# First transfer in two steps, last row but one halved, last row as 512, 256, 256, one semaphore for two sums

## The chip, the cores and the metric

One core of one Trainium2 chip. The time is the device time of one execution in microseconds (us), a median over executions. The profile covers a *span*: from the start of the first recorded instruction of the program to the end of its last. The device time is longer than the span (by 1.35 us in the kernel before); the traces below show semaphore updates that run on after the kernel's last instruction (to 1.46 us after it). The difference between the two is called "the rest" below. A *semaphore* is a counter by which engines and transfers wait for one another, and a transfer has *landed* when its data are in the core's memory (read here from the first instruction on it). Results list spans to 0.1 us, so a single value of the rest is good to about 0.05 us.

## The reference

```
x: (32, 512, 1024) float32
out[b, s] = sum over d of max(x[b, s, d], 0)        # (32, 512) float32
```

67.1 MB are read and 0.07 MB are written, with one comparison and one addition per element.

## The kernel before

The input is seen as 128 partitions by 128 rows of 1024 elements. Seven transfers of 16 rows (8 MiB) come through three buffers. Then 8, 4, 2 and 1 rows come, and at the end the last row in three pieces. For transfers 0 to 5 ScalarE applies relu in place to a step of several rows, and VectorE sums the step with one reduction. For transfer 6 and the tail the two engines take whole rows alternately; each computes relu and sum in one instruction with an accumulator.

```python
STEPS = [4, 5, 7]            # rows of a step, transfers 0 to 4
MIXED = [3, 4, 5]            # transfer 5; its other 4 rows are done whole
TAIL = [8, 4, 2, 1]
LAST = [576, 256, 192]       # pieces of the last row
...
    for c in range(NBIG + 1):
        if c >= NB:                                   # buffer free again?
            sp.wait_ge(s_dve, 3 * (c - NB + 1))
        ...                                           # sp.dma_start(transfer c)
...
    for c in range(NTWO):                             # relu on ScalarE, sum on VectorE
        b, steps = c % NB, STEPS if c < NTWO - 1 else MIXED
        act.wait_ge(s_in[c], 16)
        ...
        for i, n in enumerate(steps):
            t = buf[:, b, r : r + n, :]
            act.activation(t, t, AF.Relu).then_inc(s_act, 1)
            dve.wait_ge(s_act, 3 * c + i + 1)
            dve.tensor_reduce(out=res[...], in_=t, axis=X, op=ALU.add).then_inc(s_dve, 1)
...
    for r, n, s in tail:                              # whole rows, alternately
        if n > 1:
            act.wait_ge(s, 16)
        dve.wait_ge(s, 16)
        for i in range(r, r + n):
            f = on_act if (i - r) % 2 else on_dve
            f(buf[:, tb, i, :], res[:, j0 + i : j0 + i + 1])

    n = LAST[2]
    act.wait_ge(s_in[-3], 16)
    on_act(parts[0], last[:, n : n + 1]).then_inc(s_tact, 1)
    dve.wait_ge(s_in[-2], 16)
    on_dve(parts[1], last[:, n + 1 : n + 2]).then_inc(s_tpart, 1)
    dve.wait_ge(s_tpart, 1)
    dve.wait_ge(s_in[-1], 16)
    dve.wait_ge(s_tact, 1)
    on_dve(last[:, :], res[:, J - 1 : J]).then_inc(s_tdve, 1)   # third piece + both sums
```

Of the kernel before, what the change touches and what calls it, by code (L numbers as in the profile page):

```python
# [2 lines left out]

P = 128
D = 1024
BIG = 16
NTWO = 6
NB = 3
REGIONS = [112, 16]
CHUNKS = [(0, 0), (0, 16), (0, 32), (0, 48), (0, 64), (0, 80), (0, 96)]  # L10
STEPS = [4, 5, 7]
MIXED = [3, 4, 5]
TAIL = [8, 4, 2, 1]
LAST = [576, 256, 192]


def bass_relu_sum_kernel(
    nc: bass.Bass,
    x: bass.AP,
    out: bass.AP,  # L20
):







    fp32 = mybir.dt.float32
    ALU = mybir.AluOpType  # L30
    AF = mybir.ActivationFunctionType
    X = mybir.AxisListType.X

    B, S, _ = x.shape
    J = B * S // P
    NBIG = len(CHUNKS)
    assert BIG * NBIG + sum(TAIL) + 1 == J == sum(REGIONS) and sum(LAST) == D

    xr = x.rearrange("b s d -> (b s) d")
    of = out.rearrange("b s -> (b s)")  # L40
    start = [sum(REGIONS[:i]) for i in range(len(REGIONS))]
    xv = [
        xr[P * s : P * (s + n), :].rearrange("(p j) d -> p j d", p=P)
        for s, n in zip(start, REGIONS)
    ]
    ov = [of[P * s : P * (s + n)].rearrange("(p j) -> p j", p=P) for s, n in zip(start, REGIONS)]

    buf = nc.alloc_sbuf_tensor("buf", [P, NB, BIG, D], fp32)
    last = nc.alloc_sbuf_tensor("last", [P, LAST[2] + 2], fp32)
    res = nc.alloc_sbuf_tensor("res", [P, J], fp32)  # L50

    n_in = NBIG + len(TAIL) + len(LAST)
    s_in = [nc.alloc_semaphore(f"s_in{i}") for i in range(n_in)]
    s_act = nc.alloc_semaphore("s_act")
    s_dve = nc.alloc_semaphore("s_dve")
    s_fact = nc.alloc_semaphore("s_fact")
    s_fdve = nc.alloc_semaphore("s_fdve")
    s_tact = nc.alloc_semaphore("s_tact")
    s_tpart = nc.alloc_semaphore("s_tpart")
    s_tdve = nc.alloc_semaphore("s_tdve")  # L60
    s_store = nc.alloc_semaphore("s_store")
    s_out = nc.alloc_semaphore("s_out")

    sp, act, dve = nc.sync, nc.scalar, nc.vector


    tb = NBIG % NB


    code = nc.main_func.blocks[0].instructions  # L70
    arrival = next(
        i
        for i, ins in enumerate(code)
        if ins.engine == mybir.EngineType.SP and type(ins).__name__ == "InstDrain"
    )
    for c in range(NBIG + 1):
        if c >= NB:
            sp.wait_ge(s_dve, 3 * (c - NB + 1))
        if c < NBIG:
            g, j = CHUNKS[c]  # L80
            sp.dma_start(out=buf[:, c % NB, :, :], in_=xv[g][:, j : j + BIG, :]).then_inc(
                s_in[c], 16
            )
        if c == 0:
            code.insert(arrival, code.pop())
    r = 0
    tail = []
    for i, n in enumerate(TAIL):
        sp.dma_start(out=buf[:, tb, r : r + n, :], in_=xv[-1][:, r : r + n, :]).then_inc(  # L89
            s_in[NBIG + i], 16  # L90
        )
        tail.append((r, n, s_in[NBIG + i]))
        r += n
    n0, n1 = LAST[0], LAST[0] + LAST[1]
    parts = [buf[:, tb, r, 0:n0], buf[:, tb, r, n0:n1], last[:, 0 : LAST[2]]]
    for k, (lo, hi) in enumerate([(0, n0), (n0, n1), (n1, D)]):
        sp.dma_start(out=parts[k], in_=xv[-1][:, BIG - 1, lo:hi]).then_inc(
            s_in[NBIG + len(TAIL) + k], 16
        )
    sp.wait_ge(s_fact, 1)  # L100
    sp.wait_ge(s_fdve, 1)
    for g in range(len(REGIONS) - 1):
        sp.dma_start(
            out=ov[g][:, :], in_=res[:, start[g] : start[g] + REGIONS[g]]
        ).then_inc(s_store, 16)


    def on_act(t, acc):
        return act.activation(t, t, AF.Relu, accum_out=acc)  # L109

    def on_dve(t, acc):
        return dve.tensor_scalar(  # L112
            out=t, in0=t, scalar1=0.0, scalar2=None, op0=ALU.max, op1=ALU.add, accum_out=acc
        )

    def row(c, i):
        return buf[:, c % NB, i, :], res[:, c * BIG + i : c * BIG + i + 1]

    for c in range(NTWO):
        b, steps = c % NB, STEPS if c < NTWO - 1 else MIXED  # L120
        act.wait_ge(s_in[c], 16)
        if steps is MIXED:
            dve.wait_ge(s_in[c], 16)
            for i in (BIG - 4, BIG - 3):
                on_dve(*row(c, i))
        r = 0
        for i, n in enumerate(steps):
            t = buf[:, b, r : r + n, :]
            act.activation(t, t, AF.Relu).then_inc(s_act, 1)  # L129
            dve.wait_ge(s_act, 3 * c + i + 1)  # L130
            dve.tensor_reduce(  # L131
                out=res[:, c * BIG + r : c * BIG + r + n], in_=t, axis=X, op=ALU.add
            ).then_inc(s_dve, 1)
            r += n
        if steps is MIXED:
            for i in (BIG - 2, BIG - 1):
                on_act(*row(c, i))


    j0 = NBIG * BIG  # L140
    for c in range(NTWO, NBIG):
        act.wait_ge(s_in[c], 16)
        dve.wait_ge(s_in[c], 16)
        for i in range(BIG):
            ins = (on_act if i % 2 else on_dve)(*row(c, i))
            if i >= BIG - 2:
                ins.then_inc(s_fact if i % 2 else s_fdve, 1)
    for r, n, s in tail:
        if n > 1:
            act.wait_ge(s, 16)  # L150
        dve.wait_ge(s, 16)
        for i in range(r, r + n):
            f = on_act if (i - r) % 2 else on_dve
            f(buf[:, tb, i, :], res[:, j0 + i : j0 + i + 1])

    n = LAST[2]
    act.wait_ge(s_in[-3], 16)
    on_act(parts[0], last[:, n : n + 1]).then_inc(s_tact, 1)
    dve.wait_ge(s_in[-2], 16)
    on_dve(parts[1], last[:, n + 1 : n + 2]).then_inc(s_tpart, 1)  # L160
    dve.wait_ge(s_tpart, 1)
    dve.wait_ge(s_in[-1], 16)
    dve.wait_ge(s_tact, 1)  # L163
    on_dve(last[:, :], res[:, J - 1 : J]).then_inc(s_tdve, 1)


    sp.wait_ge(s_tdve, 1)
    sp.dma_start(out=ov[-1][:, :], in_=res[:, start[-1] : J]).then_inc(s_out, 16)
    sp.wait_ge(s_store, 16 * (len(REGIONS) - 1))
    sp.wait_ge(s_out, 16)  # L170


# [1 line left out]
_INS = ['x']  # L174
_OUTS = [((32, 512), 'float32')]


# [21 lines left out]
```

## Time and profile before

| what | value | where it is read |
|---|---|---|
| device time | 161.24 us (161.21 to 161.25, 3 executions) | results |
| span | 159.88 us | trace |
| the rest, time less span, same execution | 161.23 - 159.88 = 1.35 us | worked out |
| share of the input queue | 97.9% of 16 DMA engines' span | page, DMA queues |
| landing of the seventh transfer | 137.94 us | timeline, first instruction on it |
| last store issued | 158.41 us | timeline |

The stream of input fills the DMA engines (97.9% of their span).

The timeline of the kernel before from 156.3 us (start, duration, engine, line, operation, output and input, in square brackets the idle time before it and what ended it):

```profile
156.32 1.22 DVE L112 TENSOR_SCALAR_CACHE_REDUCE buf<-buf 128x1024 f32<-128x1024 f32 x1
157.08 0.68 ACT L109 ACTIVATE buf<-buf 128x576 f32<-128x576 f32 x1 [0.90 <-DMA buf<-in_x_dram]
157.47 0.08 DVE L112 DVE_READ_ACCUMULATOR buf<-buf 128x1 f32 x1
157.47 0.41 DVE L112 TENSOR_SCALAR_CACHE_REDUCE buf<-buf 128x256 f32<-128x256 f32 x1
157.67 0.19 ACT L109 ACTIVATION_READ_ACCUMULATOR buf<-buf 128x1 f32 x1
157.81 0.08 DVE L112 DVE_READ_ACCUMULATOR buf<-buf 128x1 f32 x1
158.02 0.36 DVE L112 TENSOR_SCALAR_CACHE_REDUCE last<-last 128x194 f32<-128x194 f32 x1
158.30 0.08 DVE L112 DVE_READ_ACCUMULATOR last<-last 128x1 f32 x1
158.41 0.34 SPq L168 DMA_DIRECT2D out_dram<-res  x1
```

And the last pieces of the chain of waits (start, duration, what):

```profile
122.28 34.02 DMA buf<-in_x_dram
156.30 0.02 issue
156.32 1.57 DVE buf L112 x4
157.89 0.01 issue
157.90 0.05 DVEq L163
157.95 0.07 issue
158.02 0.36 DVE last L112 x2
```

What to see: the last row but one is worked on by VectorE alone for 1.15 us while ScalarE is idle for 0.90; then the sums of the first two pieces end at 157.86 (ScalarE) and 157.89 (VectorE), a separate wait instruction follows at 157.90, and the last addition starts at 158.02.

### The profile page before, as it was taken

The numbers are of one execution on the slowest core, as the hardware profiler recorded it, in microseconds if no ns is written. First come the engines' busy times: TensorE is split into PE (matmuls) and PEld (weight loads), VectorE is DVE, ScalarE is ACT, GpSimd is POOL, SyncE is SP. The second block draws the span as 40 slices with busy tenths as digits, with TensorE's granted clock in tenths as the row PEclk, the third lists the DMA queues.
The fourth block names the chain that finished last, engine by engine and source line by source line (L and its number), as shares of the span: only waits on it lengthen the run. The fifth ranks groups of instructions, "written<-read, shape, count | busy, mean of one in ns | idle before, by whom it ended". The sixth has DMA issues, their size and how long they took to land.

```text
span 159.9 us, 148 instructions
## 1 busy us (share of the span) xinstructions
DVE 122.0 (76%) x58; ACT 101.0 (63%) x55; POOL 0.2 (0%) x4
## 2 busy tenths in 40 slices
DVE  0000006989879897998969989699899999598995
ACT  3000059990699808996099941999339980496972
POOL 0000000000000000000000000000000000000000
DMA  7996996996996997989979969969969969899993
GB/s 262 525 525 262 525 525 262 525 525 262 525 492 295 525 459 328 525 377 410 525 312 476 525 262 525 525 262 525 525 262 525 525 262 525 385 402 394 414 407 116
DMA packets 2305, 67.18 MB, mean 420 GB/s; under 512 B 512, under 2 KB 768, under 8 KB 1024
## 3 DMA queue, kind: packets, MB, share of 16 engines
q1 hardware_dynamic: 2304, 67.18, 97.9%
q14 instruction: 1, 0.01, 0.0%
HBM read 67.11 MB, written 0.07 MB: 420 GB/s over the span
## 4 chain that ended last, share of the span: by engine, by line
DMA 69%; ACT 18%; DVE 11%; SPq 1%; issue 0%; DVEq 0%
DMA buf<-in_x_dram 69%; ACT buf L129 18%; DVE res L131 10%; DVE buf L112 1%; SPq L89 1%; DVE last L112 0%; DVEq L163 0%
## 5 line engine op out<-in xcount | busy, mean ns | idle before, releaser
L131 DVE TENSOR_REDUCE res<-buf 128x4 f32<-128x4096 f32 (+3 forms) x18 | 100.4, 5604 | 33.6 <-ACT buf L129 33.6
L129 ACT ACTIVATE buf<-buf 128x4096 f32<-128x4096 f32 (+3 forms) x18 | 80.8, 4553 | 46.3 <-DMA buf<-in_x_dram 46.3
L109 ACT ACTIVATE buf<-buf 128x1024 f32<-128x1024 f32 (+1 forms) x18 | 18.4, 1024 | 9.8 <-DMA buf<-in_x_dram 9.8
L112 DVE TENSOR_SCALAR_CACHE_REDUCE buf<-buf 128x1024 f32<-128x1024 f32 (+1 forms) x19 | 21.3, 1173 | 2.7 <-DMA buf<-in_x_dram 2.5
L109 ACT ACTIVATION_READ_ACCUMULATOR buf<-buf 128x1 f32 x18 | 3.4, 186 | 0.0
L129 ACT ACT_TABLE_LOAD x1 | 1.3, 1283 | 0.8 <-PEq L184 0.8
L112 DVE DVE_READ_ACCUMULATOR buf<-buf 128x1 f32 x19 | 1.6, 83 | 0.0
L112 DVE TENSOR_SCALAR_CACHE_REDUCE last<-last 128x194 f32<-128x194 f32 x1 | 0.4, 356 | 0.1
L184 POOL MEMSET const-bfloat16-1.0<- 128x1 bf16 x1 | 0.1, 102 | 0.0
L184 POOL MEMSET const-uint8-127<- 128x1 uint8 x1 | 0.1, 102 | 0.0
L184 POOL MEMSET const-float32-0.0<- 128x1 f32 x1 | 0.1, 100 | 0.2 <-issue 0.2
L184 POOL MEMSET const-float32-1.0<- 128x1 f32 x1 | 0.1, 99 | 0.0
L112 DVE DVE_READ_ACCUMULATOR last<-last 128x1 f32 x1 | 0.1, 83 | 0.0
## 6 DMA issues: line engine op xcount, KB each, us to landing
buf<-in_x_dram SPq DMA_DIRECT2D x1, 4096.0 KB, 26.7
buf<-in_x_dram SPq DMA_DIRECT2D x1, 2048.0 KB, 31.2
buf<-in_x_dram SPq DMA_DIRECT2D x1, 1024.0 KB, 33.2
buf<-in_x_dram SPq DMA_DIRECT2D x1, 512.0 KB, 34.0
buf<-in_x_dram SPq DMA_DIRECT2D x1, 288.0 KB, 34.3
buf<-in_x_dram SPq DMA_DIRECT2D x1, 128.0 KB, 34.1
buf<-in_x_dram SPq DMA_DIRECT2D x7, 36.3
last<-in_x_dram SPq DMA_DIRECT2D x1, 96.0 KB, 33.9
```

Of the source, the lines that this page charges most:

```text
L89: sp.dma_start(out=buf[:, tb, r : r + n, :], in_=xv[-1][:, r : r + n, :]).then_inc(s_in[NBIG + i], 16)
L109: return act.activation(t, t, AF.Relu, accum_out=acc)
L112: return dve.tensor_scalar(out=t, in0=t, scalar1=0.0, scalar2=None, op0=ALU.max, op1=ALU.add, accum_out=acc)
L129: act.activation(t, t, AF.Relu).then_inc(s_act, 1)
L131: dve.tensor_reduce(out=res[:, c * BIG + r : c * BIG + r + n], in_=t, axis=X, op=ALU.add).then_inc(s_dve, 1)
L184: nc = _bacc.Bacc("TRN2", target_bir_lowering=False, num_devices=1)
```

## The change

The intent is a shorter tail: both engines share the last row but one, so that they reach the last row's pieces earlier; the pieces are re-cut for that; the two sums count on one semaphore, so that the last instruction waits on one fewer. The first transfer goes in two steps, 7 and 9 rows, in place of three. The cuts of the diff are index arithmetic and the list of steps per transfer.

```diff
-STEPS = [4, 5, 7]
-MIXED = [3, 4, 5]
+STEPS = [[7, 9], [4, 5, 7], [4, 5, 7], [4, 5, 7], [4, 5, 7], [3, 4, 5]]
-LAST = [576, 256, 192]
+LAST = [512, 256, 256]
+    half = nc.alloc_sbuf_tensor("half", [P, 2], fp32)
-    s_tact = nc.alloc_semaphore("s_tact")
-    s_tpart = nc.alloc_semaphore("s_tpart")
+    s_half = nc.alloc_semaphore("s_half")
+    s_part = nc.alloc_semaphore("s_part")
 ...
-            sp.wait_ge(s_dve, 3 * (c - NB + 1))
+            sp.wait_ge(s_dve, done[c - NB])
 ...
+    r, _, s = tail[-1]
+    act.wait_ge(s, 16)
+    dve.wait_ge(s, 16)
+    on_act(buf[:, tb, r, 0 : D // 2], half[:, 0:1]).then_inc(s_half, 1)
+    on_dve(buf[:, tb, r, D // 2 : D], half[:, 1:2]).then_inc(s_half, 1)
+    dve.wait_ge(s_half, 2)
+    dve.tensor_tensor(
+        out=res[:, j0 + r : j0 + r + 1], in0=half[:, 0:1], in1=half[:, 1:2], op=ALU.add
+    )
 ...
-    on_act(parts[0], last[:, n : n + 1]).then_inc(s_tact, 1)
+    on_act(parts[0], last[:, n : n + 1]).then_inc(s_part, 1)
     dve.wait_ge(s_in[-2], 16)
-    on_dve(parts[1], last[:, n + 1 : n + 2]).then_inc(s_tpart, 1)
-    dve.wait_ge(s_tpart, 1)
+    on_dve(parts[1], last[:, n + 1 : n + 2]).then_inc(s_part, 1)
+    dve.wait_ge(s_part, 2)
     dve.wait_ge(s_in[-1], 16)
-    dve.wait_ge(s_tact, 1)
```

More of the change, by code (lines that the diff above doesn't have):

```diff
@@ L6 @@
 BIG = 16
-NTWO = 6
 NB = 3
@@ L64, in bass_relu_sum_kernel @@
     sp, act, dve = nc.sync, nc.scalar, nc.vector
+    NTWO = len(STEPS)
+    done = [sum(map(len, STEPS[: c + 1])) for c in range(NTWO)]
     tb = NBIG % NB
@@ L117, in row @@
         return buf[:, c % NB, i, :], res[:, c * BIG + i : c * BIG + i + 1]
-    for c in range(NTWO):
-        b, steps = c % NB, STEPS if c < NTWO - 1 else MIXED
+    k = 0
+    for c, steps in enumerate(STEPS):
         act.wait_ge(s_in[c], 16)
-        if steps is MIXED:
+        alone = BIG - sum(steps)
+        if alone:
             dve.wait_ge(s_in[c], 16)
-            for i in (BIG - 4, BIG - 3):
+            for i in range(BIG - alone, BIG - alone // 2):
                 on_dve(*row(c, i))
         r = 0
-        for i, n in enumerate(steps):
-            t = buf[:, b, r : r + n, :]
+        for n in steps:
+            t = buf[:, c % NB, r : r + n, :]
             act.activation(t, t, AF.Relu).then_inc(s_act, 1)
-            dve.wait_ge(s_act, 3 * c + i + 1)
+            k += 1
+            dve.wait_ge(s_act, k)
             dve.tensor_reduce(
@@ L134, in bass_relu_sum_kernel @@
             r += n
-        if steps is MIXED:
-            for i in (BIG - 2, BIG - 1):
-                on_act(*row(c, i))
+        for i in range(BIG - alone // 2, BIG):
+            on_act(*row(c, i))
     j0 = NBIG * BIG
@@ L147, in bass_relu_sum_kernel @@
                 ins.then_inc(s_fact if i % 2 else s_fdve, 1)
-    for r, n, s in tail:
-        if n > 1:
-            act.wait_ge(s, 16)
+    for r, n, s in tail[:-1]:
+        act.wait_ge(s, 16)
         dve.wait_ge(s, 16)
@@ L154, in bass_relu_sum_kernel @@
             f(buf[:, tb, i, :], res[:, j0 + i : j0 + i + 1])
+    r, _, s = tail[-1]
+    act.wait_ge(s, 16)
+    dve.wait_ge(s, 16)
[5 more added lines that the diff above has]
+    )
     n = LAST[2]
     act.wait_ge(s_in[-3], 16)
-    on_act(parts[0], last[:, n : n + 1]).then_inc(s_tact, 1)
+    on_act(parts[0], last[:, n : n + 1]).then_inc(s_part, 1)
     dve.wait_ge(s_in[-2], 16)
-    on_dve(parts[1], last[:, n + 1 : n + 2]).then_inc(s_tpart, 1)
-    dve.wait_ge(s_tpart, 1)
+    on_dve(parts[1], last[:, n + 1 : n + 2]).then_inc(s_part, 1)
+    dve.wait_ge(s_part, 2)
     dve.wait_ge(s_in[-1], 16)
-    dve.wait_ge(s_tact, 1)
     on_dve(last[:, :], res[:, J - 1 : J]).then_inc(s_tdve, 1)
```

## The prediction

> **What bounds the kernel.** The input stream. The DMA part of the page gives queue 1 97.9% of the sixteen engines' span. In the timeline the 8 MiB transfers land (first ScalarE instruction on each) at 21.84, 41.19, 60.54, 79.88, 99.23, 118.59 and 137.94 us: every 19.35 us, about 433 GB/s by my arithmetic. [...] The chain of waits charges 28% to the ScalarE and VectorE passes before a buffer is freed, but that is not stalling: a transfer issued at 62.9 us lands at 99.2 only because another transfer is ahead of it in the queue. So only the last 1.5 us after the stream can change.
>
> **First transfer in two steps (7, 9).** It removes one ACTIVATE and one TENSOR_REDUCE and later lets the first buffer go. Reductions take 4.418 us for 4 rows and 7.620 for 7, so 9 rows take about 9.75 (estimate). VectorE ends transfer 0 near 45.65 instead of 43.53, transfer 1 near 63.2 instead of 62.9, and has caught up at 64.18. The transfers issued at these times need to move data only from 60.5 and 79.9: over 14 us of slack. Worth 0.
>
> **The tail now** (timeline from 156 us): last row but one lands 156.30; VectorE works on it from 156.32 for 1.15 us while ScalarE is idle 0.9 us; then 256 elements 157.47 to 157.89. ScalarE does 576 elements from 157.08 and its accumulator read ends at 157.86. The third piece lands at 157.68 (issue 123.78 plus 33.9). The built order puts ScalarE's semaphore and that landing in a separate wait instruction (157.90 to 157.95), then the last VectorE instruction starts at 158.02, reads out until 158.38, store issue 158.41. So ScalarE's sum, through 0.16 us of wait instruction and issue, and VectorE's, 0.13 us earlier, both end close together; data alone would allow about 157.82.
>
> **The tail after**, estimates from these durations:
> - Slopes: VectorE 1.04 ns per element (256: 415 ns, 1024: 1216), ScalarE 0.80 (576: 684, 1024: 1044).
> - Half row: VectorE reads out by 157.0, ScalarE by 157.06.
> - The added 128x1 sum is in no trace yet. [...]
> - 512 elements land near 157.00, so ScalarE's part ends near 157.75. 256 land near 157.31, so VectorE's part ends near 157.75 instead of 157.89. Third landing unchanged, 157.68 to 157.72: the bytes are the same.
> - The separate wait now holds the landing alone, and the last instruction waits for the common semaphore itself (0.02 us from event to start elsewhere in the trace): start near 157.82 instead of 158.02, minus 0.20.
> - The last instruction has 258 elements for 194: plus 0.07.
> Net gain 0.13 us of 161.24, 0.08%.
>
> **Prediction:** 161.11 us, eight in ten between 161.00 and 161.23. Faster by over 2%: 0.3%; within 2%: 99.4%; slower by over 2%: 0.3%.
>
> **What would show it right:** landings still 19.35 us apart and the seventh at 137.94; VectorE's 9-row reduction 9.75 us; the 128x1 addition at 157.1 before the 256 elements at 157.33; last instruction at 157.82 lasting 0.42 us; store issued near 158.28.
>
> **What would make it wrong:** the later release does delay the stream (landings after 79.9 shift); the small last transfers land later than I place them, since 512, 256, 256 are other descriptor sizes; the addition or its wait runs past 157.33 and holds the next VectorE instruction; landing-to-landing variation of a tenth of a microsecond hides the gain.

The forecast's sum: minus 0.20 us for the earlier start of the last instruction, plus 0.07 us for its longer piece, so minus 0.13 us on 161.24, which gives 161.11.

## More of the kernel before

From the page of the kernel before: the span, the busy time and instruction count of the two engines, and the DMA queues (packets, MB, share of sixteen engines' span).

```profile
span 159.9 us, 148 instructions
...
DVE 122.0 (76%) x58; ACT 101.0 (63%) x55; POOL 0.2 (0%) x4
...
q1 hardware_dynamic: 2304, 67.18, 97.9%
q14 instruction: 1, 0.01, 0.0%
```

## The result, and the profile after

Ratios below are the mean time of one kernel's fast runs over that of the other's of the same rounds, so not quite the ratio of the medians quoted.

| kernel | median | range | executions |
|---|---|---|---|
| before | 161.24 us | 161.20 to 161.25 | 6 |
| after | 161.49 us | 161.17 to 161.80 | 6 |

The ratio is 1.0016, with a 95% interval of 1.0002 to 1.0031: within 2%, a little slower, and outside the predicted range of 161.00 to 161.23. The six executions of the changed kernel, with their spans:

```
time   161.28  161.75  161.17  161.80  161.49  161.48
span   159.9   159.9   159.8   159.8   159.7   160.1
rest     1.38    1.85    1.37    2.00    1.79    1.38
```

The mean span is 159.87, no longer than the 159.88 of the kernel before. The mean rest is 1.63 where the kernel before had 1.35 (one execution only, but its 30 later executions have a mean of 1.36). **So the whole loss of this comparison lies outside the span**, in three of the six executions, and the profile page, which shows the first execution only, cannot show it.

The same lines of the page after:

```profile
span 159.9 us, 149 instructions
...
DVE 121.5 (76%) x58; ACT 101.5 (64%) x56; POOL 0.2 (0%) x4
...
q1 hardware_dynamic: 2304, 67.18, 97.9%
q14 instruction: 1, 0.01, 0.0%
```

Two groups of the timeline after that answer the question about the two steps (the second merges the 9-row reduction and three reductions of the next transfer):

```profile
35.92 27.06 DVE L135 TENSOR_REDUCE res<-buf 128x9 f32<-128x9216 f32 x4 [0.15 <-ACT buf L132]
...
64.29 9.85 DVE L135 TENSOR_REDUCE res<-buf 128x4 f32<-128x4096 f32 x2 [1.30 <-ACT buf L132]
```

And the tail, from 156.4 us:

```profile
156.46 0.63 ACT L111 ACTIVATE buf<-buf 128x512 f32<-128x512 f32 x1
156.46 0.69 DVE L114 TENSOR_SCALAR_CACHE_REDUCE buf<-buf 128x512 f32<-128x512 f32 x1
157.00 0.19 ACT L111 ACTIVATION_READ_ACCUMULATOR buf<-buf 128x1 f32 x1
157.07 0.08 DVE L114 DVE_READ_ACCUMULATOR buf<-buf 128x1 f32 x1
157.14 0.63 ACT L111 ACTIVATE buf<-buf 128x512 f32<-128x512 f32 x1
157.22 0.16 DVE L164 TENSOR_TENSOR res<-half 128x1 f32<-128x1 f32 x1
157.49 0.42 DVE L114 TENSOR_SCALAR_CACHE_REDUCE buf<-buf 128x256 f32<-128x256 f32 x1
157.68 0.19 ACT L111 ACTIVATION_READ_ACCUMULATOR buf<-buf 128x1 f32 x1
157.83 0.08 DVE L114 DVE_READ_ACCUMULATOR buf<-buf 128x1 f32 x1
157.95 0.42 DVE L114 TENSOR_SCALAR_CACHE_REDUCE last<-last 128x258 f32<-128x258 f32 x1
158.30 0.08 DVE L114 DVE_READ_ACCUMULATOR last<-last 128x1 f32 x1
158.41 0.34 SPq L179 DMA_DIRECT2D out_dram<-res  x1
```

What to see: VectorE is back in step at 64.29 (64.18 before, and the whole stream of this execution is 0.10 to 0.11 us later, from the first landing on). Both engines start the halved row at 156.46, the added sum takes 0.16 us, and the last VectorE instruction starts 157.95 - 138.05 = 19.90 us after the seventh landing, where before it was 158.02 - 137.94 = 20.08. It takes 0.06 us longer. The last store is issued 20.36 us after the seventh landing for 20.47: the tail gained 0.11 us. Measured from a landing, these numbers are free of the jitter of the stream's start.

### The profile page after: what moved, and what is told of

The parts are those of the page before. It is cut to its first block, busy times and chain, and to the rows that moved or that the text cites. A ratio compares the mean times of both kernels' runs of the same rounds, so it can differ in the third digit from the quotient of the medians.

```text
span 159.9 us, 149 instructions
## 1 busy us (share of the span) xinstructions
DVE 121.5 (76%) x58; ACT 101.5 (64%) x56; POOL 0.2 (0%) x4
## 4 chain that ended last, share of the span: by engine, by line
DMA 58%; DVE 22%; ACT 18%; SPq 1%; issue 0%
DMA buf<-in_x_dram 58%; DVE res L135 22%; ACT buf L132 18%; SPq L91 1%; SPq L99 0%; DVE buf L114 0%; DVE last L114 0%
## 5 line engine op out<-in xcount | busy, mean ns | idle before, releaser
L135 DVE TENSOR_REDUCE res<-buf 128x7 f32<-128x7168 f32 (+4 forms) x17 | 100.2, 5924 | 34.0 <-ACT buf L132 34.0
L132 ACT ACTIVATE buf<-buf 128x7168 f32<-128x7168 f32 (+4 forms) x17 | 80.7, 4810 | 46.5 <-DMA buf<-in_x_dram 46.5
L111 ACT ACTIVATE buf<-buf 128x1024 f32<-128x1024 f32 (+1 forms) x19 | 19.0, 1001 | 9.0 <-DMA buf<-in_x_dram 8.9
L114 DVE TENSOR_SCALAR_CACHE_REDUCE buf<-buf 128x1024 f32<-128x1024 f32 (+2 forms) x19 | 20.9, 1146 | 2.8 <-DMA buf<-in_x_dram 2.5
```

The costliest lines, as they stand in the source:

```text
L111: return act.activation(t, t, AF.Relu, accum_out=acc)
L114: return dve.tensor_scalar(out=t, in0=t, scalar1=0.0, scalar2=None, op0=ALU.max, op1=ALU.add, accum_out=acc)
L135: dve.tensor_reduce(out=res[:, c * BIG + r : c * BIG + r + n], in_=t, axis=X, op=ALU.add).then_inc(s_dve, 1)
```

## The experiments

All sixteen runs gave correct results. They ran on three chips. First theory: the loss is after the span and comes with one part of the change. Rivals: it was a disturbance of the first occasion; or a later release of the first buffer delays the stream.

### The change again, and one part at a time

`after_again`: no edit.

> The changed kernel once more, unedited. In its six runs so far the span of the profile was 159.7 to 160.1 us, like the kernel before (159.9), while the device time was 161.17 to 161.80; time less span was 1.37 to 2.0 us against 1.33. Theory A (cost outside the span, from something in the change): again 0.2 to 0.4 us slower in the median, a spread of about 0.6 us, and time less span of 1.4 to 2.0. Theory B (a disturbance of that chip or moment): times of 161.1 to 161.3 like the kernel before, with a spread under 0.1 us.

`e1_steps`: the two steps alone (the changed kernel's loop and wait counts, everything else as before).

```diff
-STEPS = [4, 5, 7]
-MIXED = [3, 4, 5]
+STEPS = [[7, 9], [4, 5, 7], [4, 5, 7], [4, 5, 7], [4, 5, 7], [3, 4, 5]]
```

> The first transfer in 7 and 9 rows, alone. Theory A1 (the loss comes with the two steps, as a stream delay or outside the span): median 161.4 to 161.6 with a spread of about 0.6 us. Rival A2 (it comes with the halved row and its added sum): 161.24 with a spread under 0.1 us. Inside the span both expect nothing: landings as before, VectorE caught up by 64.2 us.

`e2_half`: the halved row alone.

```diff
+    on_act(buf[:, tb, r, 0 : D // 2], half[:, 0:1]).then_inc(s_half, 1)
+    on_dve(buf[:, tb, r, D // 2 : D], half[:, 1:2]).then_inc(s_half, 1)
+    dve.wait_ge(s_half, 2)
+    dve.tensor_tensor(...)
```

> The halved row with the 128x1 sum, alone (576, 256, 192 and the two separate semaphores kept). Theory A2 (the added sum, an operation that VectorE had not run before, costs outside the span): median 161.4 to 161.6, spread about 0.6 us. Rival A1 (the two steps): 161.24, spread under 0.1. Inside the span, my reading that ScalarE's 576 elements through the separate wait instruction set the end: last VectorE instruction still starts 20.08 us after the seventh transfer lands, gain 0; if VectorE set it: it starts at 19.96 or earlier.

`e3_sem`: one semaphore alone.

```diff
-    dve.wait_ge(s_tpart, 1)
+    dve.wait_ge(s_part, 2)
     dve.wait_ge(s_in[-1], 16)
-    dve.wait_ge(s_tact, 1)
```

> One semaphore for both sums, alone. The separate wait instruction then holds the last landing alone and the last VectorE instruction waits for the sums itself. My reading: it starts about 0.11 us earlier against the seventh landing (19.97 instead of 20.08 us), median 161.13. Rival (the wait instruction is not on the path, VectorE's own sum is): unchanged within 0.03 us, 161.24. Spread under 0.1 us, unless the two increments to one semaphore are what costs outside the span (then 161.4 to 161.6, spread 0.6).

Measured, with 9 executions of the kernel before. "Tail" is the last store's issue less the seventh landing, in the one profiled execution. "Counts" are instructions against the kernel before, ScalarE / VectorE.

| kernel | counts | median us (range) | ratio (95%) | rest, mean (range) | tail |
|---|---|---|---|---|---|
| before | 0 / 0 | 161.23 (161.12 to 161.56) | | 1.36 (1.32 to 1.40) | 20.47 |
| after_again | +1 / 0 | 161.22 (161.11 to 161.38) | 0.9999 (0.9987 to 1.0012) | 1.39 (1.35 to 1.42) | 20.38 |
| e1_steps | -1 / -1 | 161.49 (161.42 to 161.57) | 1.0016 (1.0003 to 1.0028) | 1.60 (1.55 to 1.69) | 20.48 |
| e2_half | +2 / +1 | 161.38 (161.30 to 161.66) | 1.0013 (1.0000 to 1.0025) | 1.53 (1.30 to 1.68) | 20.45 |
| e3_sem | 0 / 0 | 161.28 (161.14 to 161.47) | 1.0001 (0.9988 to 1.0015) | 1.35 (1.31 to 1.38) | 20.41 |

(The 20.47 is from the profile; the kernel before was timed but not profiled anew.)

The changed kernel did not repeat its loss here, and neither A1 nor A2 holds alone: each part lengthens the rest (by 0.24 and 0.17 us), and with both in it the changed kernel's rest is only 0.03 longer. That speaks against a fixed cost of one part and points to something in which they cancel. The instruction counts do: the rest is at its shortest where both counts are those of the kernel before. The expected 161.24 for e2_half under A1 and the expected 0.11 us earlier start of e3_sem both failed; e3_sem's last instruction started 20.01 after the seventh landing for 20.08, 0.07 earlier. The reading of e2_half inside the span held: its last VectorE instruction started 20.07 us after the seventh landing, so ScalarE's 576 elements through the separate wait still set the end.

Past the span's end the trace holds semaphore records and instruction packets. In the kernel before, semaphore 2 is updated five times 116 to 279 ns after the end of the span. Five runs of updates start at 249 to 500 ns and end by 841; each goes upward through its own block of 51 semaphore numbers, of which 43 to 49 are in the record. Then semaphore 2 is updated nine times more, at 1105 to 1463 ns. I call the five runs "resets", and the expectations below also call the updates of semaphore 2 a "handshake" and its steps. These are names only: the record gives the number of the semaphore and the time, not the purpose. Times of three of the runs, in ns after the end of the span:

```
                  first reset of the group of semaphores       instruction packet of 8192 bytes,
                  54-104    105-155   156-206                  start (negative: inside the span)
before              346       339       303                    -192
after               342       340       306                    -195
e1_steps            343       339       851                    +1332
e2_half             655       338       304                    -313
```

In e1_steps one run of resets starts 0.55 us later, and in e2_half another one 0.31 us later. In e1_steps the instruction packet that the other three have before the end of the span is missing from the page: there is no q14 line, and it starts at +1332 instead.

```profile
span 159.9 us, 146 instructions
...
DVE 121.7 (76%) x57; ACT 100.9 (63%) x54; POOL 0.2 (0%) x4
...
q1 hardware_dynamic: 2304, 67.18, 97.8%
```

A late reset is not by itself a longer rest. In this execution of e2_half the last update of semaphore 2 comes 1450 ns after the span, for 1463 in the kernel before, and its rest, 1.30, is the lowest of its five; the other four (1.47 to 1.68) were not profiled.

### The counts alone

New theory A: what the rest costs is set by the instruction counts of ScalarE and VectorE, whatever the instructions do. The test is to add instructions that do nothing: waits on the first transfer's semaphore, long satisfied, placed ahead of the wait for the second transfer, where ScalarE idles 5.3 us. Counted in the built programs, 1, 3, 12 and 32 added waits make 1, 2, 6 and 16 instructions.

`p1_steps_act1` and `p2_steps_dve1`: on e1_steps, one instruction put back, on ScalarE or on VectorE.

```diff
+        if c == 1:
+            act.wait_ge(s_in[0], 16)      # p1; in p2: dve.wait_ge(s_in[0], 16)
         act.wait_ge(s_in[c], 16)
```

> The two steps of e1_steps, with one satisfied wait added on ScalarE (at the second transfer), so that ScalarE has as many instructions as the kernel before and VectorE one less. Theory A (the loss comes after the last store: VectorE's instruction count places its end-of-program semaphore resets later, they started 0.85 us after the span's end in e1_steps against 0.30): still slow, median 161.45 to 161.55, time less span 1.55 to 1.69. Rival B (ScalarE's count does it): back to 161.2, time less span 1.33 to 1.40. Rival C (neither count, but the later release of the buffer): 161.45 to 161.55 here and in p2 as well.

> The two steps of e1_steps, with one satisfied wait added on VectorE (at the second transfer), so that VectorE has as many instructions as the kernel before and ScalarE one less. Theory A (VectorE's count): back to 161.2, time less span 1.33 to 1.40, its resets start 0.30 us after the span. Rival B (ScalarE's count): still 161.45 to 161.55. Rival C (the later release): still 161.45 to 161.55.

`p3_before_act1` and `p4_before_act2`: the kernel before with one or two instructions more on ScalarE (the same lines, 1 and 3 waits).

> The kernel before with one satisfied wait added on ScalarE at the second transfer and nothing else: the counts of the changed kernel (ScalarE 1 more, VectorE the same). Theory A: inside the span nothing; after it what the changed kernel shows, time less span 1.35 to 1.42 in most executions and on some chips 1.8 to 2.0 in half of them; in the profile the end-of-program handshake has one step of about 0.09 us in place of 0.035. Rival D (it is the added sum or its own semaphores that lengthen the end): time less span 1.33 to 1.40 with no longer step.

> The kernel before with two satisfied waits added on ScalarE and nothing else: ScalarE's count of e2_half, VectorE's of before. Theory A: ScalarE's resets start 0.65 us after the span's end in place of 0.35, time less span 1.3 to 1.7, median 161.35 to 161.45, as e2_half. Rival D (the halved row itself, or VectorE's one more): 161.2 with time less span 1.33 to 1.40.

| kernel | counts | median us (range) | ratio (95%) | rest, mean (range) |
|---|---|---|---|---|
| before (12 executions) | 0 / 0 | 161.31 (161.14 to 161.75) | | 1.35 (1.32 to 1.40) |
| p1_steps_act1 | 0 / -1 | 161.65 (161.59 to 161.91) | 1.0017 (1.0004 to 1.0030) | 1.79 (1.69 to 1.91) |
| p2_steps_dve1 | -1 / 0 | 161.33 (161.30 to 161.71) | 1.0002 (0.9990 to 1.0015) | 1.52 (1.50 to 1.55) |
| p3_before_act1 | +1 / 0 | 161.34 (161.20 to 161.52) | 0.9998 (0.9986 to 1.0010) | 1.41 (1.37 to 1.44) |
| p4_before_act2 | +2 / 0 | 161.39 (161.17 to 161.73) | 1.0003 (0.9991 to 1.0015) | 1.56 (1.37 to 1.63) |

The device times spread by half a microsecond on this chip, for the kernel before too, because the spans do (159.8 to 160.4). So their medians decide nothing; the rest, with a spread below 0.1 us for most kernels, decides. Rival D falls with p3 and p4: one or two waits that do nothing lengthen the rest by 0.06 and 0.21. Rival C (the later release) falls with p1 and p2, which have the same release and differ by 0.27 in the rest. Theory A holds in the main, but I had one engine's part wrong: p2 did not come back to 1.35; ScalarE's missing instruction costs 0.17 by itself. And the counts do not add up: p1, with one instruction less on VectorE alone, has 1.79, above the expected 1.55 to 1.69 and above e1_steps (1.60), which lacks one on both engines. The trace of each shows a different place:

```
ns after the span  first reset   first reset   semaphore 2 after the resets: the steps that differ
                   54-104        156-206
before               346           303         1105 to 1139 (34)       1382 to 1416 (34)
p1  (0 / -1)         343           852         1171 to 1311 (140; before: 44)
p2  (-1 / 0)         348           310         1385 to 1560 (175; before: 34)
p3  (+1 / 0)         342           305         1110 to 1193 (83; before: 34)
p4  (+2 / 0)         649           305         none
after (+1 / 0)       342           306         1104 to 1191 (87; before: 34)
```

p4 differs from the kernel before by ScalarE's two waits alone, and its resets of 54-104 are late. e1_steps and p1, the two kernels so far with an instruction less on VectorE, are the two with late resets of 156-206, and p2, which puts that instruction back, is not. So I read the group 54-104 as ScalarE's and 156-206 as VectorE's. The changed kernel and p3 have the same counts and the same one step that takes 0.05 us longer. That the changed kernel's ordinary rest of 1.40 comes from ScalarE's one added instruction is thereby shown.

What lengthens the rest where resets are late: the traces show this much. In fourteen of the eighteen profiled executions the rest is the last update of semaphore 2 less 0.10 to 0.12 us, so a longer step in the table above is a longer rest. The four others are those in which an instruction packet starts 1.31 to 1.34 us after the span: p4 and e1_steps lie 0.08 to 0.09 us above that relation, n2 (below) 0.20, and p1, which alone has a second such packet (at 1.67 us), 0.50. In p4, as in e2_half, the late resets of 54-104 delay nothing: semaphore 2 ends at 1451 ns, and its profiled execution has the lowest rest of its six (1.37, the others 1.56 to 1.63). In the profiles, then, a longer rest goes with a longer step or with a late packet, and not with late resets of 54-104 alone; that the late packet causes it is not shown.

### Equal counts, three steps, and the pieces alone

`n1_equal_counts`: the changed kernel, with the second transfer in two steps as well and one satisfied wait added on VectorE, so counts of 0 / 0.

```diff
-STEPS = [[7, 9], [4, 5, 7], [4, 5, 7], ...
+STEPS = [[7, 9], [7, 9], [4, 5, 7], ...
+        if c == 1:
+            dve.wait_ge(s_in[0], 16)
```

> The changed kernel with the second transfer in two steps (7, 9) too, which takes one more instruction from ScalarE and from VectorE, and one satisfied wait added on VectorE: both engines then have as many instructions as in the kernel before. Theory A (end cost by instruction counts): time less span 1.33 to 1.40, no long step in the end handshake, and the gain of the tail stays: last store issued 20.36 us after the seventh landing in place of 20.47; median 0.10 us under the kernel before of the same chip. If the changed kernel's own operations lengthen the end instead: time less span 1.38 or more, no gain.

`n2_three_steps`: the changed kernel without the two steps.

```diff
-STEPS = [[7, 9], [4, 5, 7], [4, 5, 7], ...
+STEPS = [[4, 5, 7], [4, 5, 7], [4, 5, 7], ...
```

> The changed kernel with the first transfer in three steps like the others: ScalarE then has 2 instructions more than the kernel before and VectorE 1 more, as e2_half. Theory A: the two steps are worth nothing inside the span and keep the counts down: without them time less span is 1.3 to 1.68 and the median 0.1 to 0.25 us over the changed kernel of the same chip; ScalarE's resets start 0.65 us after the span. Rival (the two steps only cost): the same or faster than the changed kernel.

`after_third`: no edit.

> The changed kernel unedited, on this call's chip, to stand beside the two others, and to see whether the 1.8 to 2.0 us after the span of its first six executions come back. Theory A as the second and third chip showed it: time less span 1.35 to 1.45, median within 0.05 us of the kernel before. If the first chip's state is common: half of the executions at 1.8 to 2.0.

`e4_last`: on the kernel before, `LAST = [512, 256, 256]` alone.

> The last row as 512, 256, 256, alone (both semaphores and the whole last row but one kept; counts as before). Inside the span: ScalarE's sum ends near 157.75 on the clock of the kernel before, so VectorE's own sum (157.89) sets the last instruction, near 157.92, which is 0.07 us longer: last store 20.44 us after the seventh landing in place of 20.47. Time less span 1.33 to 1.40; median 0.03 us under the kernel before, lost in the spread. Rival (third piece lands later with 1024-byte rows than with 768): 20.50 or more.

| kernel | counts | median us (range), 4 executions | ratio (95%) | rest, mean (range) | tail |
|---|---|---|---|---|---|
| n1_equal_counts | 0 / 0 | 161.30 (161.26 to 161.42) | 0.9997 (0.9983 to 1.0012) | 1.34 (1.32 to 1.38) | 20.34 |
| n2_three_steps | +2 / +1 | 161.34 (161.26 to 161.39) | 0.9997 (0.9984 to 1.0010) | 1.58 (1.56 to 1.62) | 20.38 |
| after_third | +1 / 0 | 161.24 (161.14 to 161.47) | 0.9993 (0.9980 to 1.0006) | 1.40 (1.37 to 1.44) | 20.48 |
| e4_last | 0 / 0 | 161.15 (161.11 to 161.20) | 0.9987 (0.9972 to 1.0001) | 1.35 (1.31 to 1.40) | 20.45 |

The rest follows the counts again: 1.34 and 1.35 with equal counts, 1.58 for n2 with ScalarE's resets at 669 ns. So the two steps buy 1.58 - 1.40 = 0.18 us after the span, though inside it they are worth nothing: they keep the counts near those of the kernel before. (Whether that was their purpose I do not know.) The tail of n1 was as expected, its median was not: the 0.1 us gained do not show through the jitter of four executions. e4_last has the lowest median of all; its spans happened to be 159.8 in all four, its tail gained 0.02 (0.03 expected), and its interval includes 1, so it is not a faster kernel by these runs. after_third's profiled tail of 20.48 was a miss: there the third piece landed 157.68 - 137.77 = 19.91 us after the seventh transfer, for 19.74 in the kernel before.

### The place of a packet, or a cost for each instruction

Still open was whether each instruction costs (rival F), or whether it matters where an instruction packet falls (theory E): it started at -192 ns in the kernel before and at +1332 in e1_steps. The mechanism that theory E names on record is cut below, since no run shows it; what it expected stands. `q1_before_act16` and `q2_before_act6`: the kernel before with 16 or 6 satisfied wait instructions on ScalarE (32 and 12 waits, at the same place). `n3_last_and_sem` has the two parts that leave the counts alone: the pieces and the one semaphore.

> The kernel before with 16 satisfied waits added on ScalarE (in the idle time before the second transfer). Theory E [...]: [...] time less span is back to 1.33 to 1.40 and ScalarE's resets start 0.35 us after the span. Rival F (each added ScalarE instruction costs time at the end): time less span 1.6 or more. Theory E fails as well if the tail inside the span grows.

> The kernel before with 6 satisfied waits added on ScalarE. Theory E: either back to 1.33 to 1.40 already, or between 1.5 and 1.7 like the 2 added before, and ScalarE's resets start at 0.35 or at 0.65 us accordingly. Rival F (a cost for each instruction): 2 added cost about 0.22 us, 6 then about 0.6 us, time less span near 2.0.

> The changed kernel unedited, on a further chip or in a further call. Theory A with ScalarE's one added instruction on the edge: 1.37 to 1.44 us after the span as on the second and third chip, or, if the state of the first six executions returns, 1.8 to 2.0 in some.

> The kernel before with two of the four parts: 512, 256, 256 and one semaphore; no halved row, no two steps, so both engines have as many instructions as before. My reading: VectorE's own sum (ends 157.89 on the clock of the kernel before) sets the last instruction at 157.91, 258 elements take 0.07 us more: last store 20.41 to 20.43 us after the seventh landing, time less span 1.33 to 1.40, median 0.05 us under the kernel before. If the whole row but one was what held VectorE, it stays 0.05 us behind the changed kernel's 20.36.

| kernel | counts | median us (range) | ratio (95%) | span, mean | rest, mean (range) | tail |
|---|---|---|---|---|---|---|
| before (9 executions) | 0 / 0 | 161.20 (161.15 to 161.43) | | 159.88 | 1.36 (1.31 to 1.40) | |
| q1_before_act16 | +16 / 0 | 161.75 (161.59 to 161.96) | 1.0034 (1.0020 to 1.0047) | 160.38 | 1.36 (1.35 to 1.39) | 20.87 |
| q2_before_act6 | +6 / 0 | 161.82 (161.42 to 161.91) | 1.0033 (1.0021 to 1.0046) | 160.44 | 1.32 (1.31 to 1.34) | 21.06 |
| after_fourth | +1 / 0 | 161.23 (161.08 to 161.31) | 0.9999 (0.9986 to 1.0011) | 159.78 | 1.42 (1.38 to 1.45) | 20.35 |
| n3_last_and_sem | 0 / 0 | 161.32 (161.12 to 161.69) | 1.0007 (0.9994 to 1.0019) | 159.98 | 1.35 (1.32 to 1.40) | 20.45 |

Rival F (a cost for each instruction) falls: with 6 and with 16 instructions more the rest is back to 1.32 and 1.36. Theory E is half right. By the words on record it fails too, since it was to fail if the tail inside the span grew, and that grew by 0.40 and 0.59 us (20.87 and 21.06 for 20.47). What goes with it can be read. In q2 an instruction packet starts at 144.72 us, in q1 at 142.11, in the middle of the stream. q2's page has two instruction packets where the kernel before has one:

```profile
q1 hardware_dynamic: 2304, 67.18, 97.5%
q14 instruction: 2, 0.02, 0.0%
```

From there on the landings are late. ScalarE's first instruction on the 8 rows, in the kernel before and then in q2:

```profile
147.64 1.06 ACT L109 ACTIVATE buf<-buf 128x1024 f32<-128x1024 f32 x1 [1.28 <-DMA buf<-in_x_dram]
```

```profile
148.32 1.06 ACT L109 ACTIVATE buf<-buf 128x1024 f32<-128x1024 f32 x1 [1.88 <-DMA buf<-in_x_dram]
```

Each of these transfers has sixteen updates of its semaphore on record, and the kernel waits for a count of 16. The records of the last two:

```
us                     16-row transfer 6          8 rows                     last piece
                       2nd last    last           2nd last    last           2nd last    last
before                 137.88      137.91         147.60      147.62         157.64      157.68
q1 (packet at 142.11)  137.93      137.95         147.67      148.10         157.69      158.10
q2 (packet at 144.72)  137.89      138.00         147.71      148.30         157.75      158.28
```

After the packet exactly one of sixteen updates is 0.4 to 0.6 us behind, and it is still 0.41 and 0.53 behind the others at the last piece; q2's input queue fills 97.5% of the engines' span. The packet's 8192 bytes take 0.31 us in the queue's record in q1 and 0.32 in q2. Why one update of sixteen falls behind is not shown, as the trace as kept does not name the engine that a packet went through; and a lag of 0.43 and 0.59 at the 8 rows is more than the packet's own time, which stays unexplained.

n3 shows that pieces and semaphore alone do not make the tail: 20.45, not the expected 20.41 to 20.43. With the whole row but one on VectorE its own sum is what comes last: it ends at 157.77, and the last instruction starts at 157.81. (n3's median, expected 0.05 us under the kernel before, came out above it, within the noise.) The kernels with the halved row, the pieces and the one semaphore together (after, n1, n2) have 20.34 to 20.38 in five of six profiles and 20.48 in the sixth; with one profile each, e3_sem's 20.41 is not far from them.

## Why the prediction was wrong, point by point

- **The stream bounds the kernel; two steps are worth 0 inside the span: right.** Landings stayed 19.35 us apart, VectorE was back in step at the third transfer, and e1_steps has the tail of the kernel before (20.48 for 20.47). 8 MiB every 19.35 us are 433 GB/s.
- **The tail gains 0.13 us: right in mechanism, 0.02 too much.** In the first profile the last store came 20.36 us after the seventh landing for 20.47, 0.11 earlier. Over six profiles of the new tail (after four times, n1, n2) the mean is 20.38, over six of the old one (before, e1, p1 to p4) 20.49. The added sum took 160 ns; the last instruction took 422 ns. VectorE's 256 elements began at 157.49, which is 0.05 later than predicted once the execution's 0.11 us of later landings is taken off: their piece landed at 157.46, 0.04 later than predicted by the same measure, and VectorE's own sum, ending at 157.91, is what the last instruction then followed, at 157.95.
- **"So only the last 1.5 us after the stream can change": this is the step that failed.** It treated the 1.35 us between span and device time as fixed. They are not: the rest went from 1.30 to 2.00 us across these kernels, and the sum had no term for it. For the changed kernel that term is +0.05 in 14 executions on three later occasions (mean 1.40, against 1.36 in 30 executions of the kernel before), and it takes back half of the tail's gain. In the first six executions it was +0.28 (1.63 against the one 1.35), more than the gain; what made it so large there stays open (below).
- **"landing-to-landing variation of a tenth of a microsecond hides the gain": right as a warning, too small.** The kernel before itself spread over 161.12 to 161.75 in later calls. The profiles show where: the first landing lay between 21.69 and 22.14 us, and the seventh followed it 116.1 us later in every one of these kernels. What makes it vary was not examined. The range of 0.23 us was too narrow for this alone.

On the three chips the changed kernel and the kernel before are equal within the noise (ratios 0.9999, 0.9993, 0.9999, each with about 0.0013 to either side). **Open** is why the rest was 1.8 to 2.0 us in three of the first six executions. It never came back in 14 further ones, nor in the five of p3 with the same counts; p1 is the only other kernel with values near it, 1.69 to 1.91. In the changed kernel's first profile one step of semaphore 2 takes 0.05 us longer (87 ns for 34); a still longer step there is a guess of mine, and no profile caught one. Another candidate is a late instruction packet as in p1, whose profiled execution had two after the span and a rest of 1.91; no profile of the changed kernel has one.

No kernel tried beats both clear of the noise. n1_equal_counts has the best of both parts by the traces (tail 20.34, rest 1.34), about 0.1 us under the kernel before; with stream jitter of several tenths its four executions cannot show it.

## What to carry to other kernels

Where a change is worth a tenth of a microsecond, look past the end of the span: compare device time less span, and count the instructions on each engine, because in this kernel adding or removing one instruction lengthened the rest by 0.05 to 0.44 us with the same work done, while six and sixteen more did not. Test this with instructions that do nothing, which tells the work from the count; and see whether an instruction packet falls into the stream, since here, with the input queue at 97.5 and 97.6% of the engines' span, one of sixteen updates then came 0.4 to 0.6 us late and the tail was 0.40 and 0.59 us longer. Measure a tail from a landing, not from zero, so that the jitter of the stream's start drops out.
